# Finer weight units in two expert groups, and the general path moved ahead of the last up products

## The chip, the cores and the metric

The kernel runs on one core of one Trainium2 chip. The metric is the device time of one execution in microseconds (us). The kernel before takes 687.73 us, the median of three runs (687.39 to 687.77). The profiled execution took 687.93 us, and its span from the first to the last instruction is 686.2 us.

## What is computed

The reference is one decoder block on 256 tokens of width 1024 in float32: an attention and convolution mixer, cross-attention into a fixed memory, and then a mixture of 32 experts with top-1 group and top-2 expert routing, a residual and a final RMSNorm. Only the experts matter here:

```python
def expert_step(y, args):
    wg, wu, wd, ge = args
    out = (jax.nn.silu(t @ wg) * (t @ wu)) @ wd
    return y + ge[:, None] * out, None

y, _ = lax.scan(expert_step, jnp.zeros_like(t), (w_gate, w_up, w_down, gates))
...
x = x + y
return rmsnorm(x, final_g)
```

Each of the 32 experts has a gate matrix and an up matrix of 1024 x 512 and a down matrix of 512 x 1024, 2 MB each, so the experts' weights are 201 MB.

## The kernel before

**Experts in groups of four.** `NGR` = 8 groups run one after the other. A group gathers for each of its four experts up to 32 tokens (`gather`, which writes `tg`), multiplies them by the gate weights (`eg`) and the up weights (`eu`) of the four experts, the four in column groups of 32 of the same PSUM bank, forms `silu(eg) * eu`, turns the result round (`hidden_T`: transposes into `hTp` on TensorE, then a copy `hT<-hTp` on ScalarE), multiplies by the down weights (`ed`) and adds the tokens' rows into four PSUM banks `Yp`. Every product of an expert has two instructions in the profile. The last group (g = 7) has no ordinary down part: `finale` does the down products in three column slices (`SLICES`), adds the residual `X` (through an identity matrix, L1164 and L1169), normalises and stores.

**Weights come through a ring.** `Ring` hands out 25 slots of 1 MB in 15 blocks, some of one slot and some of two. `queue` lists the loads in their order, and `pump`, called from `done`, issues the next loads as soon as the slots that their turn needs are free (L139, all on SyncE's queue, SP). A load of 2 MB needs a whole block of two slots. All gate and up weights are loads of 2 MB, one expert each with 16 KB in a row per partition, except group 0's gate: that comes in eight units (m, k) of 1 MB, rows 2m and 2m+1 of two experts, with 4 KB in a row. The ordinary products run with the contraction index j outside and the expert q inside (L1328 to L1331), so all but the first three products of a matrix wait for the fourth expert's load. The last group's down weights are cut finer: ("ed", 7, 0, 0) and (0, 1), then (1, 0), (2, 0), (3, 0), (1, 1), (2, 1) of 1 MB each, and (3, 1) in two halves of 0.5 MB. They are the last weights of the stream.

**Eight counters.** In the built program every load has one of eight counters, DMAHW0 to DMAHW7 in turn (called lanes here). A load raises its counter by 16 when it has landed, and the queue that issues it waits first until the load eight before it, on the same counter, has landed.

**The general path.** No more than 32 tokens of an expert fit a group; what is left over goes through `overflow`: every engine reads the count `ntot` (L1115) and branches (L1116). With these inputs the count is zero and the loop is not entered. The loop would issue six DMAs on SP. Where it is not entered, the built program has every engine raise its own counter by what the loop would have added, and SP raises the counters of the six lanes, each by 16: it waits until the last load on that lane has landed, adds 16, and goes to the next lane (L1116 on SP, in the order 0, 1, 2, 5, 6, 7). So what stands behind `overflow` and uses these counters finds them as if the loop had run.

**Order.** A scheduler puts the instructions of each engine in order, except inside `manual_schedule`; nothing is moved across the branch. Ahead of the branch in the kernel before stand group 7's up products and `hidden_T`. The final gain is broadcast into a ring slot by a DMA on ScalarE's queue (L1343): in the source it stands just ahead of `overflow`, and the scheduler put it behind group 6's `hT` copy.

Of the kernel before, what the change touches and what calls it, by code (L numbers as in the profile page):

```python
# [21 lines left out]
P = 128  # L22
D = 1024
S = 256
NT = S // P
# [152 lines left out]

SLICES = [(0, 512), (512, 256), (768, 256)]


def body(tc, a, out):
# [133 lines left out]
            ring.queue(("mo", c, h), (4, 512), wmov[:, 4 * h:4 * h + 4, 512 * c:512 * c + 512])  # L318
    for g in range(NE // 4):
        for kind, w in (("eg", w_gate), ("eu", w_up)):  # L320
            if (kind, g) == ("eg", 0):

                for m in range(4):
                    for k in range(2):
                        wv = w[2 * k:2 * k + 2].rearrange("q (p j) f -> p q (j f)", j=NJ)
                        ring.queue((kind, 0, m, k), (2, 2 * DE), wv[:, :, 2 * DE * m:2 * DE * (m + 1)])
                continue
            for q in range(4):
                ring.queue((kind, g, q), (NJ, DE), w[4 * g + q].rearrange("(p j) f -> p j f", j=NJ))
        last = g == NE // 4 - 1  # L330
        if not last:
            for q in range(4):
                wv = w_down[4 * g + q].rearrange("(p j) n -> p j n", j=4)
                for h in range(1 if q < 2 else 2):
                    ring.queue(("ed", g, q, h), (4 if q < 2 else 2, D), wv if q < 2 else wv[:, 2 * h:2 * h + 2])
        if last:

            wv = w_down[4 * g:4 * g + 4].rearrange("q (p j) n -> p j q n", j=4)
            for k in range(2):
                ring.queue(("ed", g, 0, k), (2, D), wv[:, 0, 2 * k:2 * k + 2, :])  # L340
            for j, n in [(1, 0), (2, 0), (3, 0), (1, 1), (2, 1)]:
                ring.queue(("ed", g, j, n), (4, 512), wv[:, j, :, 512 * n:512 * n + 512])
            c0, w = SLICES[1]
            ring.queue(("ed", g, 3, 1), (4, 512), wv[:, 3, :, c0:c0 + w])
            c0, w = SLICES[2]
            ring.queue(None, (4, w), wv[:, 3, :, c0:c0 + w], (("ed", g, 3, 1), slice(256, 512)))
# [764 lines left out]

    def overflow(ntot, eidx, thr):

        ow, slots = zip(*[ring.spare((SLOT,)) for _ in range(3)])
        nv = nc.values_load(ntot[0:1, 0:1], min_val=0, max_val=NITEM)  # L1115
        with tc.If(nv > 0):  # L1116
            with tc.For_i(0, nv, 1) as it_:
                er = nc.values_load(eidx[0:1, ds(it_, 1)], min_val=0, max_val=NE - 1)
                kv = mo.tile([P, NT, 1], F32, tag="kc", name="okv")
                gv = mo.tile([P, NT, 1], F32, tag="gc", name="ogv")  # L1120
                V.tensor_copy(kv, key[:, :, ds(er, 1)])
                V.tensor_copy(gv, GT[:, :, ds(er, 1)])
                V.tensor_tensor(kv, kv, thr[:, ds(it_, 1)].unsqueeze(1).to_broadcast([P, NT, 1]), op=OP.subtract)
                small_ = ow[2]
                Sv, SR = pick_mats(kv, CAP, G, small_[:, 0:NT * CAP].rearrange("p (i t) -> p i t", i=NT))
                tg = new_tg(CAP)
                gather(SR, CAP, tg)
                GST = put_back(gate_mats(Sv, gv, CAP), CAP,
                               small_[0:CAP, 256:256 + NT * P].rearrange("p (i t) -> p i t", i=NT))
                pgu = []  # L1130
                for w in (w_gate, w_up):
                    o = e_ps("oo")
                    for h in range(2):
                        wt_ = ow[h].rearrange("p (j f) -> p j f", j=4)
                        nc.sync.dma_start(wt_, w[ds(er, 1)].rearrange("o (p j) f -> p (o j) f", j=NJ)[:, 4 * h:4 * h + 4])
                        for jj in range(4):
                            j = 4 * h + jj
                            T.matmul(o[0:CAP], tg[:, j], wt_[:, jj], start=j == 0, stop=j == NJ - 1,
                                     tile_position=(0, 0))
                    pgu.append(o)  # L1140
                hh = hidden_T(pgu[0], pgu[1], CAP, small_[0:CAP, 512:512 + DE],
                              small_[:, 1024:1024 + 4 * CAP].rearrange("p (j t) -> p j t", j=4))
                yd = new_yd(CAP)
                for n in range(2):
                    o = e_ps("od")
                    wt_ = ow[n].rearrange("p (j f) -> p j f", j=4)
                    nc.sync.dma_start(wt_, w_down[ds(er, 1)].rearrange("o (p j) n -> p (o j) n", j=4)[
                        :, :, 512 * n:512 * n + 512])
                    for j in range(4):
                        T.matmul(o[0:CAP], hh[:, j], wt_[:, j], start=j == 0, stop=j == 3, tile_position=(0, 0))  # L1150
                    combine(o, CAP, GST, yd[:, n], Ycols(512 * n, 512), 512)
# [2 lines left out]

    fin = {}

    def finale(g, hh, GST):
        Z, gain_, junk = fin["Z"], fin["g"], fin["junk"]
        ss, part, r = [keep.tile([P, NT, 4], F32, name="f" + k) for k in ("ss", "part", "r")]
        yd = new_yd(P).rearrange("p a b -> p (a b)")  # L1160
        os_ = [e_ps("ed") for _ in SLICES]

        for i in range(NT):
            T.matmul(Yp[i][1], ident, X[:, i, 512:], start=False, stop=True)  # L1164
            V.tensor_copy(X[:, i, 512:], Yp[i][1])

        def begun(n, i, bank):
            c0, w = SLICES[n]
            T.matmul(bank[:, :w], ident, X[:, i, c0:c0 + w], start=True, stop=False)  # L1169
# [129 lines left out]
    V.tensor_add(GT, GT, G2)  # L1299
    state = (tg0, gate_mats(S0, quad(GT, 0), P))  # L1300

    def first_gate(o, tg):

        with tc.manual_schedule(engines={mybir.EngineType.PE}):
            for m, (j0, j1) in enumerate([(2, 3), (3, 5), (5, 7), (7, 8)]):
                gather(SR0, P, tg, j0, j1, j1 - j0)
                ws = [ring.take(("eg", 0, m, k)) for k in range(2)]
                for j in (2 * m, 2 * m + 1):
                    for q in range(4):
                        T.matmul(o[32 * q:32 * q + 32], tg[:, j, 32 * q:32 * q + 32],  # L1310
                                 ws[q // 2][0][:, q % 2, DE * (j % 2):DE * (j % 2 + 1)],
                                 start=j == 0, stop=j == NJ - 1, tile_position=(0, 32 * q))
                for _, pool in ws:
                    ring.done(pool)

    NGR = NE // 4
    table = None
    for g in range(NGR):
# [3 lines left out]
        for kind in ("eg", "eu"):  # L1322
            o = e_ps(kind)
            if (kind, g) == ("eg", 0):
                first_gate(o, tg)
            else:
                ws = [ring.take((kind, g, q)) for q in range(4)]
                for j in range(NJ):  # L1328
# [2 lines left out]
                                 start=j == 0, stop=j == NJ - 1, tile_position=(0, 32 * q))  # L1331
                ring.done(*[units for _, units in ws])
            pgu.append(o)
        GST = GST or put_back(GS, P)
        hh = hidden_T(pgu[0], pgu[1], P)
        last = g == NGR - 1
# [2 lines left out]
            for i in range(NT):  # L1339
                T.matmul(Yp[i][0], ident, X[:, i, 0:512], start=False, stop=False)  # L1340
        if last:
            fin["g"] = ring.spare((D,))[0]
            nc.scalar.dma_start(fin["g"], a["final_g"].partition_broadcast(P))  # L1343
            fin["Z"] = ring.spare((NT, D))[0]
            fin["junk"] = ring.spare((NT, D))[0]
            overflow(*table)
            finale(g, hh, GST)
            break
        yd = new_yd(P)
# [42 lines left out]
```

## Time and profile before

| what | value |
|---|---|
| median of three runs | 687.73 us |
| profiled execution | 687.93 us |
| its span | 686.2 us |
| TensorE busy | 573.4 us, 84% of the span |
| DMA, HBM read | 235.70 MB, 345 GB/s over the span |
| packets of SP's queue | 86.4% of 16 engines' span |
| mean granted TensorE clock | 0.926 |

The table has shares over the whole span. It says that neither TensorE nor the DMA engines are busy all the time, but not when. The kernel has two halves: about 240 us of dense layers, in which the DMA engines have gaps, and then the experts, in which the weights stream in at a steady rate. Which of the two limits a stretch is read from windows, and what ends the kernel from the chain of waits.

### The profile page before, as it was taken

The page shows a single profiled execution, that of the slowest core. Times are in us where ns is not written, and L with a number is a line of the kernel's source. Part 1 is how long each engine was busy: PE and PEld are TensorE (multiplying, and loading weights), DVE is VectorE, ACT ScalarE, POOL GpSimd, SP SyncE. Part 2 cuts the span into 40 slices and gives each one's busy share as a digit, 9 for nine tenths or more (in the row PEclk, how much of TensorE's full clock was granted, in tenths as well). Part 3 has the DMA queues.
Part 4 walks back from the last instruction along what each step waited for, and adds up shares of the span by engine and source line. Part 5 has one row for each costly group of instructions (what it writes and reads, how often), then busy time and mean ns, then how long its engine had stood idle before and what let it go on. Part 6 is the DMA issues. An engine that isn't in the chain of part 4 may idle for free. (4 is left out here: it accounts for less than half of the span.)

```text
span 686.2 us, 8698 instructions
## 1 busy us (share of the span) xinstructions
PE 573.4 (84%) x3497; PEld 343.3 (50%) x3497; DVE 222.4 (32%) x488; ACT 173.4 (25%) x377; POOL 119.2 (17%) x106
## 2 busy tenths in 40 slices
PE   7999999998999999987957857886685788678485
PEld 4999889876998752622512511341251134125032
DVE  5699879886774620400100100010010001001012
ACT  6575775574664511000000000000000000000004
POOL 4646435674434100000000000000000000000000
PEclk9999999999999999999969978996997899699789
DMA  7979613555847899999999999999999999999993
GB/s 226 333 203 360 250 59 124 183 185 183 308 135 273 350 397 413 429 420 430 428 426 419 426 428 423 430 426 423 429 425 428 416 430 426 426 426 426 418 386 110
DMA packets 55530, 237.34 MB, mean 346 GB/s; under 512 B 10668, under 2 KB 30272, under 8 KB 42432
## 3 DMA queue, kind: packets, MB, share of 16 engines
q1 hardware_dynamic: 55200, 235.72, 86.4%
q10 hardware_dynamic: 288, 1.05, 0.4%
q8 instruction: 28, 0.46, 0.3%
q14 instruction: 14, 0.11, 0.0%
HBM read 235.70 MB, written 1.05 MB: 345 GB/s over the span
## 5 line engine op out<-in xcount | busy, mean ns | idle before, releaser
L1330 PE MATMUL eu<-w,tg 128*32 128x512 f32 x512 | 96.4, 715 | 54.5 <-DMA w<-in_w_up 54.5
L430 POOL TENSOR_TENSOR WL<-w,WH 128x512 fp32r<-128x512 f32 (+1 forms) x80 | 109.3, 1376 | 110.1 <-ACT WH L428 103.3
L1356 PE MATMUL ed<-w,hT 128*32 128x512 f32 x448 | 75.0, 656 | 24.4 <-DMA w<-in_w_down 19.7
L428 ACT CAST WH<-w 128x512 fp32r<-128x512 f32 (+1 forms) x120 | 72.9, 619 | 48.3 <-PE pmk L435 8.3
L1330 PEld LDWEIGHTS eu<-w,tg 128*32 128x32 f32 x512 | 20.8, 127 | 124.4 <-DMA w<-in_w_up 79.3
L1013 POOL TENSOR_SCALAR SR<-S,r 128x128 f32<-128x128 f32 x7 | 4.2, 603 | 390.8 <-PE Y L1065 339.9
L1049 DVE TENSOR_TENSOR sgm<-sgm,eu 128x512 f32<-128x512 f32 x8 | 5.5, 688 | 200.2 <-PE eu L1330 169.6
L1031 PEld LDWEIGHTS tgp<-SR,X 128*128 128x128 f32 x256 | 62.0, 335 | 12.0 <-ACT SR L1012 9.5
L1031 PE MATMUL tgp<-SR,X 128*128 128x128 f32 x256 | 63.8, 406 | 3.6 <-ACT SR L1012 3.6
L1330 PE MATMUL eg<-w,tg 128*32 128x512 f32 x448 | 56.8, 595 | 5.5 <-DMA w<-in_w_gate 5.4
L531 DVE SCALAR_TENSOR_TENSOR cacc<-z,pT,cacc 128x256 f32<-128x256 f32 x116 | 56.4, 486 | 2.6
L1356 PEld LDWEIGHTS ed<-w,hT 128*32 128x32 f32 x448 | 19.4, 115 | 75.0 <-issue 40.7
L1019 DVE TENSOR_TENSOR S<-S,GT 128x256 f32<-128x256 f32 x8 | 3.4, 425 | 123.9 <-POOL SR L1013 123.8
L1055 ACT COPY hT<-hTp 128x512 f32<-128x512 f32 x8 | 4.7, 585 | 151.3 <-PE hTp L1052 151.3
L430 DVE TENSOR_TENSOR WL<-w,WH 128x512 fp32r<-128x512 f32 (+1 forms) x40 | 36.3, 910 | 12.1 <-ACT WH L428 11.7
L1048 ACT ACTIVATE sgm<-eg 128x512 f32<-128x512 f32 x8 | 4.8, 597 | 136.8 <-PE eg L1330 120.7
L1330 PEld LDWEIGHTS eg<-w,tg 128*32 128x32 f32 x448 | 14.6, 109 | 42.3 <-issue 31.3
L1063 ACT COPY yd<-ed 128x512 f32<-128x512 f32 x14 | 8.2, 585 | 91.3 <-PE ed L1356 91.3
L1032 DVE TENSOR_TENSOR tg<-tgp,g_norm_ffn_g 128x512 f32<-128x512 f32 (+2 forms) x19 | 11.5, 607 | 53.0 <-PE tgp L1031 53.0
L1065 PE MATMUL Y<-yd,GST 128*128 128x512 f32 x56 | 25.9, 605 | 0.0
L434 PE MATMUL pmk<-w,WH 128*128 128x256 f32 x64 | 18.7, 293 | 0.0
L435 PE MATMUL pmk<-w,WH 128*128 128x256 f32 x64 | 18.7, 292 | 0.0
(352 smaller groups left out, 969.3 us busy)
## 6 DMA issues: line engine op xcount, KB each, us to landing
w<-in_w_up SPq DMA_DIRECT2D x32, 2048.0 KB, 34.3
w<-in_w_gate SPq DMA_DIRECT2D x28, 2048.0 KB, 29.5
w<-in_w_down SPq DMA_DIRECT2D x35, 1024.0 KB, 30.5
w<-in_w_down SPq DMA_DIRECT2D x14, 2048.0 KB, 38.6
w<-in_w_mkv SPq DMA_DIRECT2D x8, 1024.0 KB, 12.9
w<-in_w_gate SPq DMA_DIRECT2D x8, 1024.0 KB, 5.2
w<-in_w_in SPq DMA_DIRECT2D x7, 1024.0 KB, 8.0
w<-in_w_out SPq DMA_DIRECT2D x4, 1024.0 KB, 5.0
```

The lines of the kernel that those rows point to most:

```text
L428: A.copy(hi, src)
L430: (V if nsplit[0] % 3 == 0 else G).tensor_tensor(lo, src, hi.bitcast(F32), op=OP.subtract)
L434: T.matmul(o, L[0], R[0], start=first, stop=False)
L435: T.matmul(o, L[0], R[1], start=False, stop=False)
L531: V.scalar_tensor_tensor(dst, z[:, cb, t:t + S], pT[:, 4 * t + cb:4 * t + cb + 1], acc, op0=OP.mult, op1=OP.add)
L1031: T.matmul(t[:, j], X[:, i, ja + j::NJ], SR[:, i], start=i == 0, stop=i == NT - 1)
L1032: V.tensor_tensor(tg[:, ja:ja + step], t, gff[:, ja:ja + step].unsqueeze(2).to_broadcast([P, step, n]), op=OP.mult)
L1049: V.tensor_mul(sg, sg, pu[0:n])
L1063: ins = A.copy(yd[:, :w], pd[0:n, :w])
L1065: T.matmul(outs[i], GST[:, i], yd[:, :w], start=first, stop=last)
L1330: T.matmul(o[32 * q:32 * q + 32], tg[:, j, 32 * q:32 * q + 32], ws[q][0][:, j], start=j == 0, stop=j == NJ - 1, tile_position=(0, 32 * q))
L1356: T.matmul(os_[n][32 * q:32 * q + 32], hh[:, j, 32 * q:32 * q + 32], w[:, 512 * n:512 * n + 512], start=j == 0, stop=j == 3, tile_position ...
```

## The change

**Units.** A table `FINE` names the matrices that are loaded in units of 1 MB (two of the eight row blocks, two experts each): group 0's gate as before, and now also group 1's gate and the last group's up weights. Their products run per unit (`two_rows`), and the units' slots are given back after each pair of row blocks.

**Order.** `overflow`, the final gain's DMA and the residual's products into the right half of `Yp` (`close_sum`, L1163 and L1164 of the new file) move from behind the last group's `hidden_T` to between that group's gate and up products. `overflow` holds four ring slots instead of three, since its gathered tokens and its result no longer use the tiles `tg` and `yd`.

```diff
+FINE = [("eg", 0), ("eg", 1), ("eu", NE // 4 - 1)]
...
         for kind, w in (("eg", w_gate), ("eu", w_up)):
-            if (kind, g) == ("eg", 0):
+            if (kind, g) in FINE:
 
                 for m in range(4):
                     for k in range(2):
-                        wv = w[2 * k:2 * k + 2].rearrange("q (p j) f -> p q (j f)", j=NJ)
-                        ring.queue((kind, 0, m, k), (2, 2 * DE), wv[:, :, 2 * DE * m:2 * DE * (m + 1)])
+                        wv = w[4 * g + 2 * k:4 * g + 2 * k + 2].rearrange("q (p j) f -> p q (j f)", j=NJ)
+                        ring.queue((kind, g, m, k), (2, 2 * DE), wv[:, :, 2 * DE * m:2 * DE * (m + 1)])
...
     def overflow(ntot, eidx, thr):
 
-        ow, slots = zip(*[ring.spare((SLOT,)) for _ in range(3)])
+        ow, slots = zip(*[ring.spare((SLOT,)) for _ in range(4)])
...
-                tg = new_tg(CAP)
+                tg = small_[:, 1280:1280 + NJ * CAP].rearrange("p (j t) -> p j t", j=NJ)
...
-                yd = new_yd(CAP)
+                yd = ow[3][0:CAP, 0:D].rearrange("p (n f) -> p n f", n=2)
...
+    def close_sum():
+
+        for i in range(NT):
+            T.matmul(Yp[i][1], ident, X[:, i, 512:], start=False, stop=True)
+            V.tensor_copy(X[:, i, 512:], Yp[i][1])
+
     def finale(g, hh, GST):
...
-        for i in range(NT):
-            T.matmul(Yp[i][1], ident, X[:, i, 512:], start=False, stop=True)
-            V.tensor_copy(X[:, i, 512:], Yp[i][1])
-
...
+    def two_rows(kind, g, m, o, tg):
+        ws = [ring.take((kind, g, m, k)) for k in range(2)]
+        for j in (2 * m, 2 * m + 1):
+            for q in range(4):
+                T.matmul(o[32 * q:32 * q + 32], tg[:, j, 32 * q:32 * q + 32],
+                         ws[q // 2][0][:, q % 2, DE * (j % 2):DE * (j % 2 + 1)],
+                         start=j == 0, stop=j == NJ - 1, tile_position=(0, 32 * q))
+        ring.done(*[units for _, units in ws])
+
...
             if (kind, g) == ("eg", 0):
                 first_gate(o, tg)
+            elif (kind, g) in FINE:
+                for m in range(4):
+                    two_rows(kind, g, m, o, tg)
             else:
...
             pgu.append(o)
+            if (kind, g) == ("eg", NGR - 1):
+                overflow(*table)
+                fin["g"] = ring.spare((D,))[0]
+                nc.scalar.dma_start(fin["g"], a["final_g"].partition_broadcast(P))
+                fin["Z"] = ring.spare((NT, D))[0]
+                fin["junk"] = ring.spare((NT, D))[0]
+                close_sum()
         GST = GST or put_back(GS, P)
         hh = hidden_T(pgu[0], pgu[1], P)
         last = g == NGR - 1
...
         if last:
-            fin["g"] = ring.spare((D,))[0]
-            nc.scalar.dma_start(fin["g"], a["final_g"].partition_broadcast(P))
-            fin["Z"] = ring.spare((NT, D))[0]
-            fin["junk"] = ring.spare((NT, D))[0]
-            overflow(*table)
             finale(g, hh, GST)
             break
```

**TensorE, end of the last group's up products.** In the kernel before, with the branch behind them (`hTp` are the transposes of `hidden_T`; names in brackets are the counters that an instruction waits for):

```order
L1330 MATMUL eu<-w,tg 32x512 [waits DMAHW0_49,PE_49]
L1330 MATMUL eu<-w,tg 32x512 [waits DMAHW1_49]
L1330 MATMUL eu<-w,tg 32x512 [waits DMAHW2_49]
L1330 MATMUL eu<-w,tg 32x512 [waits DMAHW3_49]
L1330 MATMUL eu<-w,tg 32x512 x28
L1052 MATMUL hTp<-ident,sgm 128x128 [waits DVE_49]
L1052 MATMUL hTp<-ident,sgm 128x128 x3
L1115 TENSOR_LOAD ntot [waits DVE_49]
L1116 COMPARE_AND_BRANCH
```

The same products in the changed kernel, behind the branch and the residual's products:

```order
L1119 UNCONDITIONAL_BRANCH [waits PE_49,PE_sequencer_49]
L1163 MATMUL Y_3020<-X,ident 128x512
L1163 MATMUL Y_3022<-X,ident 128x512
L1310 MATMUL eu<-w,tg 32x512 [waits DMAHW3_49,DVE_49,PE_49]
L1310 MATMUL eu<-w,tg 32x512
L1310 MATMUL eu<-w,tg 32x512 [waits DMAHW4_49]
L1310 MATMUL eu<-w,tg 32x512 x5
L1310 MATMUL eu<-w,tg 32x512 [waits DMAHW5_49]
```

The branch and the residual's products now stand ahead of the up products, and these wait for one unit after the other.

**ScalarE, around the final gain's DMA.** In the kernel before it stands behind group 6's `hT` copy, ahead of the branch; the last row here is the last group's `hT` copy:

```order
L1055 COPY hT<-hTp 128x512 [waits DVE_49,PE_49]
L1343 DMA w<-in_final_g 128x1024 [waits DMAHW6_49,DMAHW4_49,PE_49]
L1063 COPY yd<-ed 128x512 [waits PE_49,Activation_49]
L1063 COPY yd<-ed 128x512 [waits PE_49]
L1012 ACTIVATE SR<-S,r_2751 128x128 [waits PE_49,Activation_49,Pool_49]
L1048 ACTIVATE sgm<-eg 128x512 [waits PE_49,Activation_49]
L1055 COPY hT<-hTp 128x512 [waits DVE_49,PE_49]
```

In the changed kernel, from the end of the branch on:

```order
L1119 UNCONDITIONAL_BRANCH [waits Activation_49,Activation_sequencer_49]
L1346 DMA w<-in_final_g 128x1024 [waits DMAHW2_49,DMAHW4_49,DMAHW0_49,PE_49]
L1058 COPY hT<-hTp 128x512 [waits DVE_49,PE_49]
L1189 COPY yd<-ed 128x512 [waits PE_49,Activation_49]
L1240 ACT_TABLE_LOAD
```

The DMA moved from ahead of the branch to behind it, directly ahead of the last group's `hT` copy, and it waits for other lanes.

**SyncE, the last loads and the branch.** In the changed kernel (the loads are the last group's down weights (1, 1), (2, 1) and the two halves of (3, 1); each row's lane is the one that it waits for):

```order
L139 DMA w<-in_w_down 128x4x512 [waits DMAHW0_49]
L139 DMA w<-in_w_down 128x4x512 [waits DMAHW1_49]
L139 DMA w<-in_w_down 128x4x256 [waits DMAHW2_49]
L139 DMA w<-in_w_down 128x4x256 [waits DMAHW3_49]
L1118 TENSOR_LOAD ntot [waits DVE_49]
L1119 COMPARE_AND_BRANCH
```

In both kernels SP comes to the branch behind its last load. With eight more loads the lanes have turned: the path that does not enter the loop now raises lanes 0, 1, 4, 5, 6 and 7, in this order. The counts that the final gain's DMA asks for are 384 on lane 0 and 368 on lane 4. The loads ahead of the branch bring these lanes to 368 and 352, and the missing 16 of each are what SP adds on that path.

## Rows read from the trace of the kernel before

**Rows 1.** Chain that ended last: start us, length us, what; whole chain's beginning and end.

```profile
663.79 1.96 PE Y L1164 x4
665.75 1.86 PE ed L1175 x24
667.61 1.06 PE Y L1169 x4
...
669.10 0.38 issue
669.48 3.65 PE ed L1175 x40
...
675.47 1.48 PE ed L1175 x24
676.95 0.02 issue
676.97 0.38 ACT yd L1185
...
681.50 0.39 DVEq L1388
```

**Rows 2.** Timeline of TensorE: start us, length us, engine, line, instructions, idle before.

```profile
642.63 1.41 PE L1330 MATMUL eu<-w,tg 128*32 128x512 f32 x2 [2.74 <-DMA w<-in_w_up]
647.54 1.91 PE L1330 MATMUL eu<-w,tg 128*32 128x512 f32 x2 [3.50 <-DMA w<-in_w_up]
652.48 9.20 PE L1330 MATMUL eu<-w,tg 128*32 128x512 f32 x58 [3.03 <-DMA w<-in_w_up]
```

**Rows 3.** Windows: stretch and length, busy of five engines, clock, DMA share, GB/s.

```profile
250.00:265.00 15.00, 15.00 (x120) 6.12 (x116) 0.72 (x2) 0.60 (x1) 0.00 (x0) 1.00 0.95 376
265.00:300.00 35.00, 33.73 (x232) 16.39 (x232) 8.54 (x26) 2.75 (x5) 0.61 (x1) 1.00 1.01 429
625.00:642.50 17.50, 13.36 (x90) 7.17 (x89) 1.72 (x3) 0.60 (x1) 0.00 (x0) 1.00 1.01 426
642.50:645.00 2.50, 1.41 (x2) 0.14 (x2) 0.00 (x0) 0.00 (x0) 0.00 (x0) 0.64 1.00 426
...
652.50:655.00 2.50, 2.50 (x12) 0.58 (x16) 0.00 (x0) 0.00 (x0) 0.00 (x0) 0.50 1.02 397
655.00:657.50 2.50, 2.50 (x20) 0.69 (x16) 0.00 (x0) 0.00 (x0) 0.00 (x0) 0.63 1.04 393
657.50:665.00 7.50, 6.14 (x41) 2.19 (x34) 0.76 (x2) 0.58 (x1) 0.00 (x0) 1.00 1.04 386
```

**Rows 4.** SyncE's instructions of the branch's line, in three stretches: first and last start.

```profile
L1116 SPq EVENT_SEMAPHORE  x2: 17/17/17, 665.8 to 665.9; - x2
...
L1116 SPq EVENT_SEMAPHORE  x1: 17/17/17, 668.4 to 668.4; - x1
...
L1116 SPq EVENT_SEMAPHORE  x4: 17/17/17, 671.1 to 671.3; - x4
```

**Rows 5.** The last load of the down weights: its issue, and from issue to landing.

```profile
L139 SPq DMA_DIRECT2D w<-in_w_down x1: 2584/2584/2584, 662.2 to 662.2; - x1
...
DMA to landing us min/median/max: 11.8/11.8/11.8
```

**Rows 6.** The final gain's DMA on ScalarE's queue: duration ns, first and last start.

```profile
L1343 ACTq EVENT_SEMAPHORE  x1: 38/38/38, 602.5 to 602.5; - x1
L1343 ACTq DMA_DIRECT2D w<-in_final_g x1: 376/376/376, 615.5 to 615.5; - x1
```

**Rows 7.** Timeline of ScalarE: the copies round that DMA, and the last `hT` copy.

```profile
617.22 0.59 ACT L1063 COPY yd<-ed 128x512 f32<-128x512 f32 x1 [14.19 <-PE ed L1356]
...
663.30 0.58 ACT L1055 COPY hT<-hTp 128x512 f32<-128x512 f32 x1 [22.73 <-PE hTp L1052]
```

**Rows 8.** Page, DMA queues (packets, MB, share of 16 engines) and DMA issues.

```profile
q10 hardware_dynamic: 288, 1.05, 0.4%
...
w<-in_w_up SPq DMA_DIRECT2D x32, 2048.0 KB, 34.3
```

**Rows 9.** Timeline of SyncE's queue: issues round group 1's gate.

```profile
237.65 1.28 SPq L139 DMA_DIRECT2D w<-in_w_down  x3
251.30 7.33 SPq L139 DMA_DIRECT2D w<-in_w_gate  x4
265.12 1.79 SPq L139 DMA_DIRECT2D w<-in_w_up  x4
```

More of the change, by code (lines that the diff above doesn't have):

```diff
@@ L1306, in first_gate @@
                 gather(SR0, P, tg, j0, j1, j1 - j0)
[L1307 to L1314, printed above, removed]
+                two_rows("eg", 0, m, o, tg)
     NGR = NE // 4
```

## The prediction

> **What bounds the kernel now.** I read the windows first, then the chain of waits, then single queues. From 265 us on the DMA engines are busy all the time and move 426 to 429 GB/s [rows 3]: from there to the last weights the stream of loads sets the pace, and TensorE waits for it. In the last group it waits for the second, third and fourth expert's up weights, until 642.63, 647.54 and 652.48 us [rows 2], 4.9 us apart, which is what 2 MB take. When the fourth is there, 58 of the matrix's 64 instructions are still to do, and they take 9.20 us. Then the chain takes over [rows 1]. From 663.79 us it runs on TensorE almost without a gap: the residual's products (1.96 us), the down products and the sums to 676.95, and from there 9.2 us of ScalarE, VectorE, stores and the end.
>
> The loads end before that. SP's bookkeeping behind the branch shows when single loads land: it passes lane 0 at 665.9, lane 1 at 668.4 and lane 2 at 671.1 us [rows 4]; these are the down weights (3, 0), (1, 1) and (2, 1) of the kernel before. The last half unit was issued at 662.2 and took 11.8 us [rows 5]: it landed at 674.0. So TensorE comes 9 us late out of the up products, and it ends 2.9 us behind the last weights. That is about all that earlier up products can give.
>
> **The units of the up weights.** The last unit is 16 of 64 instructions instead of 58, so the products end about 2.5 us (16/58 of 9.20) after the last landing, at 655 us, and the transposes `hTp` by about 657. In the kernel before these ended at 663.3 us, when the `hT` copy began [rows 7]. By themselves the units gain some 6 us for the beginning of the down products. This is cover, not gain: what comes next decides, and that is the `hT` copy on ScalarE.
>
> **The order on ScalarE.** The final gain's DMA now stands ahead of this copy on the same queue, and it waits for lane 0 at 384 and lane 4 at 368. No load brings the lanes there, only SP's bookkeeping behind the branch. SP passes lane 0, lane 1 and lane 4, in this order, each when its last load has landed. Lane 1 is now the down weights (2, 1), whose landing the kernel before shows as the pass of its lane 2: 671.1 us [rows 4]. Lane 4 is long there by then. So the DMA can't be issued before about 671 us, and the copy behind it must wait too, if ScalarE's queue holds at a DMA that waits. The trace has such a place: in the kernel before, the queue came to this DMA at 602.5 us and issued it at 615.5, and the copy behind it ran at 617.22 [rows 6, 7]. But that copy also waited for down products, so the row doesn't exclude that it could have passed. The Trainium skill (DMA: Bandwidth & Descriptors, Anatomy of one DMA) says that the DMA engines never wait for semaphores and that the issuing sequencer does so before it dispatches. By that rule the copy is held; no run here shows the other case.
>
> **When (2, 1) lands.** Three things shift it.
> - Group 1's gate. Before, its first load waited until 251.30 us, behind three loads of 237.65 [rows 9], and in 250 to 265 us the engines moved 376 GB/s, against 429 after it [rows 3]: 15 x (1 - 376/429) = 1.9 us lost. With units of one slot the first needs no slot of group 0, and the others are free by the half matrix, so this gap closes. But the rows are now 4 KB instead of 16 KB. The loads of the last down weights, which begin with such rows, ran at 397 GB/s and with 2 KB rows at 386, the engines as busy as ever [rows 3]. Group 1's gate is 8.39 MB: 21.1 us at 397 and 19.6 at 429, +1.6. Together -0.3; bounds -1.9 and +1.6.
> - The last up weights, 4 x 2 MB [rows 8]: 21.1 us at 397 instead of 19.7 at 426, +1.4; bounds 0 (as fast as the large ones) and +2.0 (as slow as 386). I take 397, the nearest in form.
> - The final gain leaves the stream ahead of the last weights. Its queue carried two transfers of 0.52 MB in 0.4% of the span [rows 8]: 1.4 us each, -1.4.
>
> The sum is -0.3, so (2, 1) lands at 670.8 us; bounds 667.8 and 673.3. The Trainium skill (DMA: Bandwidth & Descriptors, Measured) gives 341 GB/s for a transfer of 1 MB and asks for larger ones. By that figure both matrices would take 24.6 us, 5.0 us more than before each, and the end would lie some 7 us later than I forecast. The trace speaks against it: loads of 1 MB one behind the other held 386 to 397.
>
> **From there to the end.** The DMA's issue takes 0.38 us [rows 6], the copy 0.58 [rows 7], with 0.1 between them: `hT` is there at 671.9. The first down product began at 665.75 before, and from it to the end were 686.2 - 665.75 = 20.45 us [rows 1]. The products of L1169 into `Y` (1.06 us) now run ahead of `hT`, which leaves 19.4. All weights but the last two halves are there, and these land before they are needed, so the 0.38 us gap at 669.10 is the only one that may go. The gain's DMA finds an emptying queue and has about 8 us until VectorE first reads it.
>
> TensorE's clock is a term too. It stood at full speed while products ran, fell in 642.5 to 645 us, when TensorE waited, and was at 0.50 when the last matrix's products began at 652.48. They ran at 0.50 up to 655, at a mean of 0.63 in the next 2.5 us and at 1.00 from 657.5 on [rows 3]. 0.50 is 1.2 GHz and 1.00 is 2.4, so a mean of 0.63 is 1.85 us at the lower level and the rest at full speed: with the 2.5 us before, 4.4 us at half speed, in which 2.2 us of work were lost. In the changed kernel TensorE is idle from 657 to 671.9, longer than any of these waits, so the down products begin at 1.2 GHz too, and I add 2.2 us; bounds 0 (it rises at once) and 2.8.
>
> Sum: 671.9 + 19.4 + 2.2 = 693.5 us of span. Around the span lie 687.93 - 686.2 = 1.7 us, and the profiled execution is 0.2 us above the median: 695.0 us, 7.3 us slower. The residual's products and the branch, 1.96 us and a few tenths, are indeed gone from the end of the chain; they are lost behind the new wait.
>
> **The rivals.**
> - *The copy isn't held* (the DMA's wait stays off ScalarE's queue, or the semaphores are met early). Then `hT` is there at 657.5, and the down products follow the loads. The last half lands at 674.0 - 0.3 = 673.7; after it come 8 instructions of 256 columns, 0.4 us at full clock and 0.9 at half, and then the 9.2 us of the present end, up to 1 us longer at the half clock. 683.5 us of span, 684.8 at worst; 685.2 to 686.5 us, I say 685.9, faster by 0.3%. For it: the last chain shows 2.9 us behind the last weights. Against: the order of the queue. It decides if the `hT` copy begins before the gain's DMA.
> - *Held, but at full clock or released earlier.* Without the clock's term 692.8; with the gap wholly won and the up weights as fast as before, 692.0 with the clock's term.
> - *The stream slows down.* If units of 1 MB cost what the page says, 702. If they cost what 2 KB rows cost, and group 1's gap isn't won, about 697.5.
> - *The change does less than it says*: the end is bound as before by the chain, and only the branch and the residual's products go, 2.4 us off; it needs the up products to end as late as now, which 16 instead of 58 instructions exclude.
>
> **How the numbers follow.** Forecast, held and restarted at 1.2 GHz: 0.70. Held, without the clock's term or released earlier: 0.14. Held, with a slower stream: 0.07. Not held: 0.07. Something that ends near the present time: 0.02. The predicted time is that of the first, 695.0 us. The range from 692.0 to 697.5 holds the first three but for their far ends, some 0.85. A measurement of this kernel can tell about 0.2% from no change, 1.4 us. Faster by more: 0.06, for the rival that isn't held lies mostly beyond that bound; within: 0.03; slower: 0.91.
>
> **What would show it.** In the changed kernel's trace the final gain's DMA on ScalarE starts at 670 to 672 us, within 0.1 us of SP's bookkeeping, the `hT` copy within half a microsecond behind it, and the transposes ended more than 10 us earlier. TensorE stands idle between, and its clock is 0.50 for the first 4 us after that. The chain leads back over `hT` and the gain's DMA, not over TensorE. DMA moves about 397 GB/s while the up units run, and no gap is left at 250 us. I am wrong if the copy runs before the DMA, or if (2, 1) lands outside 668 to 673 us.

## The result, and the profile after

| kernel | median, us | lowest to highest | runs |
|---|---|---|---|
| before | 687.6 | 687.39 to 687.77 | 4 |
| changed | 693.8 | 692.93 to 695.85 | 4 |

The ratio is 1.0095, with a 95% interval from 1.0072 to 1.0118: the change costs 6.2 us. The profiled execution of the changed kernel took 692.93 us, of which its span is 691.2; it is the fastest of the four.

The chain of waits that ended last is short and begins late (start us, length us, what):

```profile
668.82 0.04 ACTq L1346
668.86 0.04 issue
668.90 0.38 ACTq L1346
...
669.38 0.59 ACT hT L1058
669.98 0.04 issue
670.02 3.64 PE ed L1179 x24
673.66 1.04 PE yl L1173 x2
674.70 3.58 PE ed L1179 x40
...
686.64 0.39 DVEq L1399
```

L1346 is the final gain's DMA on ScalarE's queue, and L1058 the `hT` copy behind it. The timeline of the same stretch (start us, length us, engine, line, instructions; in brackets how long the engine had stood idle, and what ended it) shows what was ready by then:

```profile
644.95 1.91 PE L1310 MATMUL eu<-w,tg 128*32 128x512 f32 x12 [1.50 <-DMA w<-in_w_up]
...
650.08 3.20 PE L1310 MATMUL eu<-w,tg 128*32 128x512 f32 x12 [1.51 <-DMA w<-in_w_up]
653.21 1.49 PE L1173 MATMUL Y<-X,ident 128*128 128x256 f32 x4
654.53 0.64 PE L1055 MATMUL hTp<-ident,sgm 128*128 128x128 f32 x4
668.90 0.38 ACTq L1346 DMA_DIRECT2D w<-in_final_g  x1
669.38 0.59 ACT L1058 COPY hT<-hTp 128x512 f32<-128x512 f32 x1 [31.99 <-DMA w<-in_w_down]
670.02 3.64 PE L1179 MATMUL ed<-w,hT 128*32 128x512 f32 x24 [14.85 <-ACT hT L1058]
```

The units do their part: after the last landing 12 products of `eu` remain where 58 did [rows 2], and the transposes `hTp` end at 655.2 us. Then no engine computes for 14 us. The copy needs only `hTp`, yet the trace puts ScalarE's 31.99 us of idle time ahead of it down to a load of down weights. That is the row to stop at: a copy from PSUM has no business with `w_down`. The load releases not the copy but the DMA ahead of it. SyncE's instructions of the branch's line, in two stretches, show when (number of instructions; ns; first and last start):

```profile
L1119 SPq EVENT_SEMAPHORE  x1: 17/17/17, 666.0 to 666.0; - x1
...
L1119 SPq EVENT_SEMAPHORE  x5: 17/17/17, 668.7 to 669.0; - x5
```

At 668.7 SP passes lane 1, on which the down weights (2, 1) count, and directly behind it lane 4; at 668.8 ScalarE's wait for the gain ends, and the DMA is issued 0.1 us later. In the kernel before, this landing stood at 671.1 [rows 4], and the chain that ended last shows no wait for it [rows 1].

The windows (stretch and length, busy time of PE, PEld, DVE, ACT and POOL, granted clock of TensorE, DMA share, GB/s) show the stream and the clock:

```profile
250.00:265.00 15.00, 14.95 (x118) 6.14 (x110) 0.93 (x3) 0.60 (x1) 0.00 (x0) 1.00 1.02 409
...
620.00:642.50 22.50, 20.43 (x132) 10.44 (x134) 3.10 (x5) 0.60 (x1) 0.00 (x0) 1.00 1.01 409
645.00:652.50 7.50, 5.33 (x28) 0.99 (x28) 0.00 (x0) 0.00 (x0) 0.00 (x0) 0.87 1.03 408
...
657.50:665.00 7.50, 0.00 (x0) 0.00 (x0) 0.00 (x0) 0.00 (x0) 0.00 (x0) 0.50 1.04 386
665.00:670.00 5.00, 0.00 (x0) 0.00 (x0) 0.00 (x0) 0.59 (x1) 0.00 (x0) 0.50 0.92 308
670.00:675.00 5.00, 4.98 (x30) 1.65 (x34) 0.00 (x0) 0.00 (x0) 0.00 (x0) 0.56 0.37 129
```

In the 12.5 us from 657.5 to 670 TensorE, VectorE and GpSimd do nothing and ScalarE makes one copy. TensorE's clock is granted at 0.50, that is 1.2 GHz, in the hold and through nearly all of the first 5 us behind it. The stream runs at 408 to 409 GB/s while the units of two rows come in: at 250 to 265 us that is more than before (376), at 620 to 642.5 us less (426 before, at 625 to 642.5) [rows 3].

The section on the change puts the turned lanes down to eight more loads. That is not the reason: eight loads are one full turn of eight lanes. What shifts the last loads by one lane is the gain's DMA, which takes a lane too and no longer does so ahead of them. SP's passes show it. Two kernels below separate the units from the order: with the order alone SP makes its last five passes together from 669.3 us on, as in the changed kernel (five from 668.7), and with the units alone its last four from 670.2 us on, as in the kernel before (four from 671.1 [rows 4]):

```profile
L1119 SPq EVENT_SEMAPHORE  x5: 17/17/17, 669.3 to 669.6; - x5
...
L1119 SPq EVENT_SEMAPHORE  x4: 17/17/17, 670.2 to 670.4; - x4
```

### The profile page after: what moved, and what is told of

Its sections match the earlier page's. It is cut to its first block, busy times and chain, and to the rows that moved or that the text cites. A ratio compares the mean times of both kernels' runs of the same rounds, so it can differ in the third digit from the quotient of the medians.

```text
span 691.2 us, 8710 instructions
## 1 busy us (share of the span) xinstructions
PE 574.6 (83%) x3497; PEld 343.7 (50%) x3497; DVE 223.4 (32%) x488; ACT 173.3 (25%) x377; POOL 119.0 (17%) x106
## 5 line engine op out<-in xcount | busy, mean ns | idle before, releaser
L1339 PE MATMUL eu<-w,tg 128*32 128x512 f32 x448 | 82.2, 717 | 44.5 <-DMA w<-in_w_up 44.5
L1339 PEld LDWEIGHTS eu<-w,tg 128*32 128x32 f32 x448 | 17.9, 127 | 104.5 <-DMA w<-in_w_up 63.9
L1339 PE MATMUL eg<-w,tg 128*32 128x512 f32 x384 | 50.4, 614 | 4.1 <-DMA w<-in_w_gate 4.1
L1058 ACT COPY hT<-hTp 128x512 f32<-128x512 f32 x8 | 4.7, 586 | 161.2 <-PE hTp L1055 129.2
L1339 PEld LDWEIGHTS eg<-w,tg 128*32 128x32 f32 x384 | 12.9, 112 | 37.1 <-issue 27.6
L1179 PE MATMUL ed<-w,hT 128*32 128x256 f32 (+1 forms) x96 | 9.2, 534 | 14.8 <-ACT hT L1058 14.8
L437 PE MATMUL pmk<-w,WH 128*128 128x256 f32 x64 | 18.7, 293 | 0.0
```

Source lines behind the costliest of these rows:

```text
L437: T.matmul(o, L[0], R[0], start=first, stop=False)
L1179: T.matmul(os_[n][32 * q:32 * q + 32, :w], hh[:, j, 32 * q:32 * q + 32], wq(q), start=j == 0, stop=j == 3, tile_position=(0, 32 * q))
```

## Experiments

My theory: the gain's DMA, which waits on ScalarE's queue, holds the `hT` copy, and that alone turns a gain into a loss. The rivals were that the units themselves make the kernel slow, that the branch or the residual's products at their new place do, and, for the size, that the clock has no part in it. Each kernel was timed against the kernel before on the same chip. Chips and times differ a little between the three batches, so only ratios are compared across them. All diffs are against the changed kernel.

**Only the gain's DMA on another queue.** The changed kernel with one word changed:

```diff
-                nc.scalar.dma_start(fin["g"], a["final_g"].partition_broadcast(P))
+                nc.sync.dma_start(fin["g"], a["final_g"].partition_broadcast(P))
```

> The changed kernel, with the final gain's DMA issued on SP's queue instead of ScalarE's; the DMA waits for the same lanes, everything else is as in the changed kernel. Theory (ScalarE's queue holds at the waiting DMA, and the hT copy behind it): the copy runs at about 655 us, right behind the transposes, the down products follow the loads, the last half unit lands at 671.5 to 672.7 us, and 9.6 to 11 us come after it: 683.5 to 685.5 us. Rival (the smaller units or the moved branch slow the end, and the wait only happens to lie beside it): about the changed kernel's 693.8 us.

Measured: 684.67 us (10 runs) against 688.79, ratio 0.9947 (0.9930 to 0.9964). ScalarE's timeline has the copy right behind the transposes:

```profile
655.29 0.58 ACT L1058 COPY hT<-hTp 128x512 f32<-128x512 f32 x1 [17.91 <-PE hTp L1055]
```

And TensorE's has the down products from 655.93 us on; from the third lot on they wait for weights:

```profile
655.93 1.93 PE L1179 MATMUL ed<-w,hT 128*32 128x512 f32 x24 [0.67 <-ACT hT L1058]
...
663.38 1.82 PE L1179 MATMUL ed<-w,hT 128*32 128x512 f32 x8 [1.68 <-DMA w<-in_w_down]
666.09 1.94 PE L1179 MATMUL ed<-w,hT 128*32 128x256 f32 x16 [0.89 <-SPq L1119]
```

The branch, the residual's products and the units stand where the change put them. So none of these makes the kernel slower than before. The same work is 0.5% faster than before with the DMA on SP's queue, and 0.95% slower with it on ScalarE's.

**The DMA stays on ScalarE, ahead of the branch.** Then nothing that it waits for hangs on SP's bookkeeping.

```diff
-                overflow(*table)
                 fin["g"] = ring.spare((D,))[0]
                 nc.scalar.dma_start(fin["g"], a["final_g"].partition_broadcast(P))
+                overflow(*table)
                 fin["Z"] = ring.spare((NT, D))[0]
```

> The changed kernel, with the final gain's DMA in front of the general path again, on ScalarE's queue as in the kernel before. Theory: no hold, as in e1, but the gain's 0.52 MB pass ahead of the last weights, so these land about 1.3 us later than in the changed kernel, and nothing is left to transfer beside the last halves: 684.5 to 686 us. Rival (the hold is of no account): 693.8 us.

Measured: 685.68 us (10 runs) against 688.79, ratio 0.9957 (0.9939 to 0.9976). ScalarE's timeline has the DMA far ahead of the copy, and the copy behind the transposes:

```profile
614.09 0.38 ACTq L1345 DMA_DIRECT2D w<-in_final_g  x1
...
656.99 0.58 ACT L1058 COPY hT<-hTp 128x512 f32<-128x512 f32 x1 [13.43 <-PE hTp L1055]
```

ScalarE's queue is harmless for this DMA at that place. What costs is the queue together with the place behind the branch.

**The units without the moved order.** Both matrices in units of two rows, the branch, the gain and the residual's products where they were before.

```diff
-            if (kind, g) == ("eg", NGR - 1):
-                overflow(*table)
-                fin["g"] = ring.spare((D,))[0]
...
+            fin["g"] = ring.spare((D,))[0]
+            nc.scalar.dma_start(fin["g"], a["final_g"].partition_broadcast(P))
...
+            overflow(*table)
+            close_sum()
```

> The finer units of both matrices, and the order of the kernel before: general path, gain's DMA and residual's products behind the last up products and their transposes. Theory: the up products end at about 653 us, and the branch and the residual's products (about 3 us) fit in front of the landing of the down weights, so the moved order brings nothing: like e2, 684.5 to 686 us. Rival (what was moved lies on the path even with early up products): 2 us slower than e2, 686.5 to 688.

Measured: 686.32 us (10 runs) against 688.79, ratio 0.9977 (0.9958 to 0.9995). The median lies just above the range of my theory and just below that of the rival. Against the kernel with the gain ahead of the branch (0.9957) the intervals overlap: what the moved branch and residual's products are worth beside the units is not settled by this pair.

**The moved order without the units.** The other half, with the gain still on ScalarE behind the branch.

```diff
-FINE = [("eg", 0), ("eg", 1), ("eu", NE // 4 - 1)]
+FINE = [("eg", 0)]
```

> The moved order alone: only group 0's gate in units of two rows, as in the kernel before. Theory (hold): the gain's DMA waits for the down weights (2, 1), which land at 671.1 less the gain's own 1.4 us, 669.7; TensorE has been idle for some 8 us by then, so the tail costs 19.4 + 2.2: 693 to 695 us, as slow as the whole change, though its up products are those of the kernel before. Rival (the units make it slow): about 687.6 us.

Measured: 693.71 us (6 runs) against 688.79, ratio 1.0083 (1.0046 to 1.0119). The timeline has the same hold with another start: here the transposes begin only at 660.38, 6 us later, and the down products again wait for the gain's DMA.

```profile
660.38 0.72 PE L1055 MATMUL hTp<-ident,sgm 128*128 128x128 f32 x4
669.55 0.38 ACTq L1346 DMA_DIRECT2D w<-in_final_g  x1
670.03 0.58 ACT L1058 COPY hT<-hTp 128x512 f32<-128x512 f32 x1 [31.26 <-SPq L1119]
670.67 3.64 PE L1179 MATMUL ed<-w,hT 128*32 128x512 f32 x24 [9.56 <-ACT hT L1058]
```

The 6 us which the units win ahead of the copy are all swallowed: the start of the down products goes by the landing of (2, 1) in both kernels.

**The hold filled.** 66 products of a constant are put on TensorE behind the last transposes; their result is not used. They change nothing but what TensorE does in the hold.

```diff
-            T.transpose(t[:, j], sg[:, j::4], ident[0:n, 0:n])
+            turned_[0] = T.transpose(t[:, j], sg[:, j::4], ident[0:n, 0:n])
...
+        if last:
+            with tc.issue_after(turned_[0].ins):
+                wm = e_ps("warm")
+                for _ in range(66):
+                    T.matmul(wm, onesb, onesb.unsqueeze(1).to_broadcast([P, 4, P]), start=True, stop=True)
```

> The changed kernel with 66 products of a constant (14 us at full clock, result unused) on TensorE between the last transposes and the first down product, that is, inside the hold. Theory (the clock's term is 2.2 us): the hold lasts as long as before, but the down products begin at full clock, so from the first down product to the end of the span pass 19.0 to 19.4 us instead of the changed kernel's 21.2, and the time is 691 to 692 us. Rival (no clock term, the tail is long for another reason): no difference from the changed kernel.

Measured: 690.88 us (5 runs) against 689.08, ratio 1.0044 (1.0021 to 1.0068). In TensorE's timeline the down products follow the filling at once:

```profile
654.89 14.41 PE L1359 MATMUL warm<-onesb 128*128 128x512 bf16 x66
669.75 1.93 PE L1181 MATMUL ed<-w,hT 128*32 128x512 f32 x24 [0.46 <-ACT hT L1060]
```

The windows, with the columns as above, grant it the full clock throughout:

```profile
665.00:670.00 5.00, 4.54 (x24) 1.92 (x26) 0.00 (x0) 0.58 (x1) 0.00 (x0) 1.00 0.92 317
670.00:675.00 5.00, 5.00 (x54) 1.76 (x50) 0.00 (x0) 0.00 (x0) 0.00 (x0) 1.00 0.32 114
```

The first 24 down products take 1.93 us instead of 3.64, and from the first of them to the end pass 688.8 - 669.75 = 19.05 us instead of 691.2 - 670.02 = 21.18. So the restart at 1.2 GHz cost 2.1 us in the changed kernel. The ratios of the two kernels, 1.0044 and 1.0095, are 3.5 us apart, with intervals that allow 2.1. The hold itself stays and with it the rest of the loss.

**The gate units taken back**, with the gain on SP in both, so that the stream decides:

```diff
-FINE = [("eg", 0), ("eg", 1), ("eu", NE // 4 - 1)]
+FINE = [("eg", 0), ("eu", NE // 4 - 1)]
...
-                nc.scalar.dma_start(fin["g"], a["final_g"].partition_broadcast(P))
+                nc.sync.dma_start(fin["g"], a["final_g"].partition_broadcast(P))
```

> e1 (gain's DMA on SP's queue) with group 1's gate in loads of 2 MB again. Theory by the traces so far: closing the gap round 250 us is worth up to 1.9 us, the bound of the prediction, so 1.2 to 1.9 us slower than e1; rival by the prediction's own sum (rows of 4 KB take back all but 0.3 us): within 0.5 us of e1.

Measured: 686.27 us (5 runs) against 689.08, ratio 0.9956 (0.9941 to 0.9971). The ratios without and with them, 0.9956 and 0.9947, are 0.6 us apart and can't be told from each other, so the times decide neither for the theory nor for its rival. The two profiles speak for the theory: counted from the beginning of the experts' loads, they take 446.5 and 445.0 us (table in the next section). The window of 250 to 265 us is back at 378 GB/s.

**The gate units alone**, in the order of the kernel before (the order edit as in the third experiment):

```diff
-FINE = [("eg", 0), ("eg", 1), ("eu", NE // 4 - 1)]
+FINE = [("eg", 0), ("eg", 1)]
```

> The kernel before with group 1's gate in units of 1 MB, and nothing else. Theory by the landings so far: the stream runs 1.2 to 1.9 us earlier from group 1 on, and the end with it: 1.2 to 1.9 us faster than the kernel before. Rival by the prediction's sum: 0.3 us, no difference that can be measured.

Measured: 687.52 us (12 runs) against 688.72, ratio 0.9979 (0.9968 to 0.9990): 0.7 to 2.2 us faster. The rival, a gain of 0.3 us as the prediction has it, lies outside.

**The gain on SP, directly behind the last load and ahead of the branch:**

```diff
-                overflow(*table)
                 fin["g"] = ring.spare((D,))[0]
-                nc.scalar.dma_start(fin["g"], a["final_g"].partition_broadcast(P))
+                nc.sync.dma_start(fin["g"], a["final_g"].partition_broadcast(P))
+                overflow(*table)
```

> The changed kernel with the gain's DMA on SP's queue directly behind the last load of the weights and ahead of the branch, so that it doesn't wait for SP's bookkeeping. In e1 the chain begins with the gain's landing at 673.24 us, issued at 669.49. Theory: the gain is issued at about 663, follows the last half on the queue and lands a few tenths earlier; the end is then bound by the down products: 0 to 0.7 us faster than e1. Rival: no difference.

Measured: 684.92 us (6 runs) against 689.08, ratio 0.9944 (0.9929 to 0.9960), the same as with the gain on SP behind the branch (0.9947). In the kernel with the gain behind the branch the chain leads over the gain's landing. When the gain comes earlier, the chain leads over down weights that land at 666.0 us and over TensorE, and the span ends at nearly the same time (682.0 and 682.1 us).

**The up weights back in loads of 2 MB**, the gate units, the moved order and the gain on SP kept:

```diff
-FINE = [("eg", 0), ("eg", 1), ("eu", NE // 4 - 1)]
+FINE = [("eg", 0), ("eg", 1)]
...
-                nc.scalar.dma_start(fin["g"], a["final_g"].partition_broadcast(P))
+                nc.sync.dma_start(fin["g"], a["final_g"].partition_broadcast(P))
```

> e1 with the last group's up weights in loads of 2 MB again, so the moved order and group 1's units alone, without the hold. Theory: the up products end at about 659 us (2 us earlier than in the kernel before by group 1's gap and the gain's bytes), hT is there at 661.5, and 19.4 us of tail at full clock follow without a wait: 681 of span, 682.5 to 684.5 us, no slower than e1, since the last weights land about 1 us earlier with rows of 16 KB. Rival (the up units are what gives the time once the hold is gone): 2 us or more slower than e1.

Measured: 682.97 us (4 runs) against 689.08, ratio 0.9905 (0.9887 to 0.9922). By the median this is the fastest kernel of the study: 6.1 us faster than before, and faster than with the up units (0.9947), with intervals that do not touch. TensorE's timeline:

```profile
650.68 9.04 PE L1339 MATMUL eu<-w,tg 128*32 128x512 f32 x58 [3.04 <-DMA w<-in_w_up]
...
662.05 1.93 PE L1179 MATMUL ed<-w,hT 128*32 128x512 f32 x24 [0.68 <-ACT hT L1058]
663.91 0.70 PE L1173 MATMUL yl<-X,ident 128*128 128x256 f32 x2
664.54 3.65 PE L1179 MATMUL ed<-w,hT 128*32 128x512 f32 x40
...
672.22 0.64 PE L1179 MATMUL ed<-w,hT 128*32 128x256 f32 x8 [0.26 <-DMA w<-in_w_down]
```

The up products end late, as in the kernel before, and the down products begin 6.1 us later than with the up units (1.2 of it since the loads began later in this execution, 238.35 against 237.10 us). The late start doesn't hold up the last of them: they wait 0.26 us for the last weights all the same. The window of 665 to 670 us in this kernel:

```profile
665.00:670.00 5.00, 5.00 (x45) 1.96 (x38) 0.00 (x0) 2.52 (x4) 0.00 (x0) 1.00 0.93 318
```

The same window in the kernel with the up units and the gain on SP:

```profile
665.00:670.00 5.00, 4.11 (x23) 1.61 (x20) 0.00 (x0) 1.87 (x2) 0.00 (x0) 0.50 0.89 305
```

Without the units TensorE does the down products of this window without a wait at 2.4 GHz. With them it does eight or sixteen at a time, stands still 0.9 to 1.7 us before three of the lots, and is granted 1.2 GHz. How much of the difference is this and how much the slower loads is not settled: in these two profiles the chain leads over the gain's landing, not over TensorE (without the up units first, then with them):

```profile
669.70 3.72 DMA w<-in_final_g
...
669.49 3.75 DMA w<-in_final_g
```

Nor do the two profiles show the whole difference. The one without the up units is the slowest of its kernel (684.10 us), the other the fastest of its own (683.86). Counted from the beginning of the experts' loads, as in the table of the next section, they are 1.0 us apart; the ratios say 2.9.

**The same with the gain behind the last load:**

```diff
-FINE = [("eg", 0), ("eg", 1), ("eu", NE // 4 - 1)]
+FINE = [("eg", 0), ("eg", 1)]
...
-                overflow(*table)
                 fin["g"] = ring.spare((D,))[0]
-                nc.scalar.dma_start(fin["g"], a["final_g"].partition_broadcast(P))
+                nc.sync.dma_start(fin["g"], a["final_g"].partition_broadcast(P))
+                overflow(*table)
```

> e8 (moved order, group 1's units, up weights in loads of 2 MB) with the gain's DMA directly behind the last load on SP's queue, as in e7. In e8 the chain begins with the gain's landing at 673.42 us, but TensorE's last product waited for the last half until 672.22. Theory: the down products bind next, so 0 to 0.7 us faster than e8, about 6 us faster than the kernel before. Rival: no difference.

Measured: 683.54 us (6 runs) against 688.72, ratio 0.9923 (0.9910 to 0.9936). It can't be told from the same kernel with the gain behind the branch (0.9905). The interval overlaps that of its counterpart with the up units (0.9929 to 0.9960) too: that the up units cost time in the new order is shown by the pair with the gain behind the branch, and this pair only points the same way.

**The moved order with the gain on SP, and no units:**

```diff
-FINE = [("eg", 0), ("eg", 1), ("eu", NE // 4 - 1)]
+FINE = [("eg", 0)]
...
-                nc.scalar.dma_start(fin["g"], a["final_g"].partition_broadcast(P))
+                nc.sync.dma_start(fin["g"], a["final_g"].partition_broadcast(P))
```

> The moved order alone, without units in either matrix, and the gain's DMA on SP's queue: e4 without the hold. Theory: the gain's bytes leave the stream ahead of the up weights (1.4 us), the branch and the residual's first products leave the way from the last up weights to the down products (in e8 11.4 us from landing to the first down product, 13.3 in the kernel before, so 1.9) and the residual's second products too (1.1): 4.2 to 4.6 us faster than the kernel before on the same chip. Rival (it is the units that give the time): within 1.4 us of the kernel before.

Measured: 685.78 us (5 runs) against 688.72, ratio 0.9959 (0.9947 to 0.9972): 2.9 us faster. The sign is right, the size was too large. Near the beginning of the chain stands the gain's landing:

```profile
670.21 3.75 DMA w<-in_final_g
```

And in TensorE's timeline the last down products wait 0.71 us for weights:

```profile
672.42 0.64 PE L1179 MATMUL ed<-w,hT 128*32 128x256 f32 x8 [0.71 <-DMA w<-in_w_down]
```

So in this execution, with the branch and the residual's products out of the end, the stream binds, and what makes the stream faster counts. The gate units are 1.5 us of it, as the next section shows. The ratios with and without them, 0.9905 and 0.9959, are 3.7 us apart; the other kernel with gate units and no up units (0.9923) is only 2.5 us away. Counted from the beginning of the experts' loads the two profiles are 1.6 to 1.7 us apart, which the gate units explain. Why the medians differ by more stays open.

## Why the prediction was right

**The mechanism.** Forecast: the copy is held by the gain's DMA, which waits for the landing of (2, 1). The trace shows the wait, the DMA within 0.1 us of SP's pass of lane 4, the copy 0.1 us behind the end of the DMA's issue, and the transposes ended 13.7 us ahead of the DMA. Moving the DMA off the queue, or off its place behind the branch, turns the sign; moving the order without the units reproduces the loss; the units without the order don't. The prediction leaned on the Trainium skill (DMA: Bandwidth & Descriptors, Anatomy of one DMA) for the queue that waits before it dispatches. The trace agrees: of the 31.99 us that ScalarE stood idle, the last 14.2 came after the transposes, with only the DMA's wait ahead of the copy. The two kernels in which nothing waits ahead of the copy (655.29 and 656.99 us) are the other case that no run showed then. One count was off without weight in the sum: behind the last landing stand 12 products, not 16, and they end at 653.3 us instead of 655, since that landing came 2.4 us earlier than before.

**The time of the hold: right mechanism, 2 us too late.** The DMA was forecast for 670 to 672 us and came at 668.90. To size the terms I take four differences. From SP's issue of group 0's last loads to the end of the wait for group 2's fourth up load, and in the last column from that issue to the end of the span. The profiled executions differ in when these loads begin (237.05 to 241.52 us); the differences leave that out.

| kernel | issue, us | wait ends, us | difference | to the end |
|---|---|---|---|---|
| before | 237.65 | 354.59 | 116.94 | 448.5 |
| moved order, no units, gain on ScalarE | 237.16 | 354.07 | 116.91 | 454.4 |
| moved order, no units, gain on SP | 237.11 | 354.28 | 117.17 | 445.7 |
| no gate units, gain on SP | 238.59 | 355.71 | 117.12 | 446.5 |
| changed | 237.13 | 352.63 | 115.50 | 454.1 |
| gain on SP | 237.10 | 352.61 | 115.51 | 445.0 |
| gain ahead of the branch | 239.03 | 354.67 | 115.64 | 446.0 |
| gate units, up loads of 2 MB, gain on SP | 238.35 | 354.04 | 115.69 | 444.0 |
| gate units alone | 238.61 | 354.21 | 115.60 | 447.2 |

The gate units are worth 115.5 - 117.0 = -1.5 us in every kernel listed that has them, and the last column has 1.3 to 1.7 us between kernels that differ in them alone. The prediction had -0.3: it won the gap of 1.9 us but charged 1.6 for rows of 4 KB at 397 GB/s. The row of 409 GB/s shows that this charge was too large: at that rate it is 0.9, which leaves -1.0. The last half microsecond stays open. The 397 came from a window of 2.5 us at the change from one form of load to another, where both may have run; no run separates them. The start of the loads, 0.5 us earlier in this execution, is another difference between two executions that no forecast holds.

From there to the release of the gain's DMA, 354.59 to 671.1 before, 354.07 to 669.4 with the moved order alone, and 352.63 to 668.8 changed: 316.5, 315.3 and 316.2 us. Taking the gain out of the stream ahead of these weights is -1.2 (forecast -1.4, half of what the gain and an output store took together), the up units +0.8 or, from the rates, 8.39 MB at 408 instead of 426 GB/s, +0.9 (forecast +1.4). Together -0.5 - 1.5 - 1.2 + 0.8 = -2.4, against 668.8 - 671.1 = -2.3; forecast -0.3. The failed step is the price of the units in the stream, the gate's above all. It lay within the bounds stated (-1.9 for the gate, 0 for the up weights).

**The end.** From the first down product to the end 21.6 us were forecast (19.4 + 2.2 for the clock), and 21.2 measured; the filled hold puts the clock's term at 2.1 and the rest at 19.05. The upper bound of 2.8 us that the prediction gave the clock is worked out from no row. The span is 2.3 us below the forecast. The median is only 1.2 below, because the profiled execution lies 0.9 below its median where that of before lay 0.2 above. That half of the miss vanishes from the median is luck.

**The rivals.** "Not held" is excluded for this change, and its price was wrong too: 1.8 us faster was forecast for it, and 4.1 us faster measured when the hold was taken away. Part of that is the same 1.2 us of the gate and 0.6 of the up units; half a microsecond stays open. "Held at full clock" is what the filled hold made, 691 us, and not what the change did. "A slower stream" fell: the windows show 408 to 409 GB/s in both places. The Trainium skill (DMA: Bandwidth & Descriptors, Measured) gives 341 GB/s for a load of 1 MB issued from GpSimd, and its rule there asks for at least 1 MiB, which these units just meet (the prediction read it as a call for larger ones). By the 341 the loads would have taken longer than before in both places; the trace does not agree.

**What the prediction did not see.** It counted 6 us of earlier up products as cover that a wait then takes away. The runs say more: in the new order the up units gain nothing even with the wait gone, since the down products then catch up with their own weights. In the order of the kernel before it is not settled: the kernels with both units and with the gate units alone have the same ratio (0.9977 and 0.9979), but their profiles, counted from the beginning of the loads, take 445.2 and 447.2 us. What was to be had in the new order lay in the order itself (2.9 us) and in the gate units (1.5 us of the stream).

## What to carry to other kernels

A DMA on a compute engine's queue is an instruction of that engine: before one is moved, ask what its wait hangs on at the new place, and what stands behind it. Waits on counters of a DMA queue can be satisfied by bookkeeping behind a branch not taken, in the order of that bookkeeping and not of the data, so a small load may inherit the landing of the last large one. Here finer loads paid where a gap held up the stream, and not where the engine that got its data earlier ran into the next load.

## What the runs showed of the hardware

- Loads of 1 MB with rows of 4 KB, one behind the other, ran at 406 to 410 GB/s at 250 to 265 us in every profile that has them there, against 423 to 429 at 265 to 300 us, where loads of 2 MB stand, and 384 to 387 at 657.5 to 665 us, where the last down weights come in rows of 2 KB.
- Four kernels with the up units, the new order and no hold made TensorE wait 0.8 to 1.7 us between lots of eight or sixteen down products. Its clock was granted at 0.50 to 0.60 over 665 to 670 us, with products in 2.6 to 4.2 of the 5 us. In the kernel with the units and the old order it stayed at 1.00, with 3.4 us of products behind waits of 1.3 and 1.6 us. I have no rule that tells these apart.
- The final gain, 0.5 MB, landed 3.7 to 4.0 us after an issue at the end of the loads. On SP's queue, with no compute behind it, an issue at 669.49 us went with a kernel faster than before (0.9947).
